# Two attentions moved from beside the branch products into the paired input products of a hybrid decoder layer

## The chip, the cores and the metric

The kernel runs on one core of a Trainium2 chip. The metric is the device time of one execution in microseconds (us); shown are the median and the extremes of three runs, and beside them one further execution that the hardware profiler recorded. Five engines work from queues of their own: PE (matrix products, with PEld for its weight loads), DVE, ACT, POOL, and SP, which here issues every DMA.

## The reference

One decoder layer on x of 1024 tokens by 1024 channels, all in fp32:

```python
h = rms_norm(x, pre_w)
(gdn_qkv, gdn_a, gdn_b, gdn_z, dq, dk, dv, dz, mq, mz, gate_logits) = [h @ w_in[:, lo:hi] for lo, hi in bounds]
...
y_gdn = oa.reshape(b, s, GDN_W).astype(x.dtype) @ w_br_gdn
...
ob = diff_attention_causal(qb, kb, vb, lam, alibi_slopes(DIFF_HEADS))
ob = rms_norm(ob, diff_norm_w) * (1.0 - lam_init)
ob = ob * jax.nn.silu(dz.reshape(b, s, DIFF_HEADS, 2 * DIFF_DH))
y_diff = ob.reshape(b, s, DIFF_W) @ w_br_diff
...
sc = jnp.einsum("bshd,bmhd->bhsm", qc, mk, preferred_element_type=f32) * (MEM_DH ** -0.5)
p = jax.nn.softmax(sc, axis=-1).astype(mv.dtype)
oc = jnp.einsum("bhsm,bmhd->bshd", p, mv).reshape(b, s, MEM_W) * jax.nn.silu(mz)
y_mem = oc @ w_br_mem
gates = jax.nn.sigmoid(gate_logits).reshape(b, s, N_BRANCH, d)
y = gates[:, :, 0] * y_gdn + gates[:, :, 1] * y_diff + gates[:, :, 2] * y_mem
return x + rms_norm(y @ w_out, post_w)
```

Differential attention has 8 heads; each takes two softmaxes (128 query rows against all earlier keys) and subtracts one from the other. Memory attention has 4 heads of 256 channels against 256 memory rows. `oa` comes from a gated delta rule, which is solved in chunks.

## The kernel before

**Stages.** To 600 us: norm of x, the delta rule with its input products, the memory's keys and values. Then `strassen`: all other columns of `h @ w_in` as 36 pairs of 128 columns. A pair is 7 products (order 1, 5, 6, 2, 7, 3, 4) of 12 matmuls 128x512; each fp32 operand is split into a high and a low part (`split`, one ACT cast and one DVE subtraction), and a product is high*high, high*low, low*high. Pair by pair come 8 key/query pairs (`key_query`), 4 of values, 4 of memory queries, 8 under Silu (`plain`, `through`) and 12 under Sigmoid. Results go to DRAM scratch. Key/query pairs also cut their result into halves and parts (`keys_apart`, `queries_apart`).

After the last pair come the branches: `branch(0)` (delta rule), during which differential heads (`diff_side`) run; then the memory heads (`mem_side`) with the heads that are left; then `branch(2)` (memory), again beside heads; `branch(1)` (differential), and the output product with its norm. A branch is 8 `gemm`s of 48 matmuls 128x512, and its 8 inputs are loaded and split (`branch_input`) before its first `gemm`.

**Steps and ticks.** Side work is written as Python generators. `count(n)` is called after n matmuls of the main work; at each `pace[0]` of them, `tick` moves every spawned generator on by one `yield`. So the source is one list of instructions with side work strewn into it, 4 matmuls apart in the branches before. A differential head works on 8 row blocks `i` of width w = 128(i+1): scores (L1051, L1052), bias and row maximum (L1054), `ng` (L1064), two Exp (L1066, L1067), the subtraction (L1069 to L1071), transposes (`turn`, L1086, copied by L1088 and L1090), and the product with the values (L1096). Block i's scores, block i-1's transposes and block i-2's value products follow one another, so three blocks are under way at a time.

**Order.** The framework that builds the kernel takes this list, chooses ahead of the run the order in which each engine gets its instructions, gives them buffers of a pool (`tag`, `bufs`), and adds the waits. Each engine then runs its own list in that order.

Of the kernel before, what the change touches and what calls it, by code (L numbers as in the profile page):

```python
# [50 lines left out]
def hybrid_layer_kernel(  # L51
# [62 lines left out]
    tri = cst([P, P], "tri")  # L114
    G.memset(tri, 1.0)
    G.affine_select(tri, tri, pattern=[[1, P]], compare_op=ALU.is_ge, fill=0.0, base=0, channel_multiplier=-1)
    mneg = cst([P, P], "mneg")
    G.memset(mneg, 0.0)
    G.affine_select(mneg, mneg, pattern=[[1, P]], compare_op=ALU.is_ge, fill=NEG, base=0, channel_multiplier=-1)
    ones = cst([P, P], "ones")  # L120
    G.memset(ones, 1.0)
# [150 lines left out]
    with ExitStack() as gx:  # L272
# [5 lines left out]
        def et(shape=(P, 512), dt=F32):  # L278
            return gp.tile(list(shape), dt, name=nm("e"), tag="e", bufs=3)

# [337 lines left out]
        def scan(h0):  # L618
# [6 lines left out]
            for c in range(8):  # L625
# [9 lines left out]
                for n, h in enumerate(hs):  # L635
                    if c:
                        V.scalar_tensor_tensor(vs[h][:, c], pa[:, n], negeG[:, h, c:c + 1], vs[h][:, c],
                                               op0=ALU.mult, op1=ALU.add)
                    if c < 7:
                        kd[h] = small([P, P], "kd", 2)  # L640
                        A.activation(kd[h], pa[:, 2 + n], AF.Copy, scale=eLG[:, h, c:c + 1])
# [4 lines left out]
                yv = small([P, 2, P], "yv", 2)  # L646
# [11 lines left out]
                for n, h in enumerate(hs):  # L658
                    if c < 7:
                        St[h] = small([P, P], f"St{n}", 2)  # L660
# [38 lines left out]
    def xtile(shape=(P, S), dt=F32):  # L699
        return xp.tile(list(shape), dt, name=nm("x"), tag="x", bufs=6)  # L700
# [3 lines left out]
    mkd = scratch("mkd", 4, (P, 4, MEM))  # L704
    mvd = scratch("mvd", 4, (P, D))
# [97 lines left out]
    class Pair:  # L803


        def __init__(self, cols, put):
            self.cols, self.put = cols, put

# [23 lines left out]
        def multiply(self, p, t):  # L832
            first = p in (1, 5, 2)
            if first:
                ps = sd().rearrange("p a b -> p (a b)")
                self.bank = {**getattr(self, "bank", {}), p: ps}
# [6 lines left out]
            if p in (1, 5, 6):  # L843
                keep = ut()
                A.copy(keep, ps)  # L845
                self.kept = {**getattr(self, "kept", {}), p: keep}
# [21 lines left out]

    def gathered(done):

        got = {}
# [12 lines left out]

    def through(func, dst):

        got = {}

        def put(i, f, ps, add):
            if i not in got:  # L890
                got[i] = xtile()
            t = got[i]
            out_ = t[:, f * 512:f * 512 + 512]
            if add is None:
                A.activation(out_, ps, func)
                A.activation(t[:, 512:], t[:, 512:], func)
            else:
                V.tensor_tensor(out_, ps, add, op=ADD)  # L898
                if i == 0 and f == 1:
                    A.activation(t, t, func)  # L900
            if (i, f) in ((0, 1), (1, 0)):
                nc.sync.dma_start(dst[i], t)
        return put

    LO, HI = slice(0, 64), slice(64, 128)
    kqd = [scratch("kqd", 6, (P, S)) for _ in range(H)]
    vd = scratch("vd", H)
    mqd = [scratch("mqd", 2, (P, S)) for _ in range(8)]
    szd = [scratch("szd", KT) for _ in range(3)]

    def keys_apart(h, t):

        for m, (a, b) in enumerate(((LO, HI), (HI, LO))):
            r = xtile(dt=F32R)
            A.copy(r[a], t[a])
            V.tensor_tensor(r[b], t[a], r[a].bitcast(F32), op=SUB)
            nc.sync.dma_start(kqd[h][m], r.bitcast(F32))
            yield

    def queries_apart(h, t):  # L920


        f = 2.0 ** (h + 1)
        for m, (a, b) in enumerate(((LO, HI), (HI, LO))):
            r = xtile(dt=F32R)
            A.activation(r[a], t[a], AF.Copy, scale=f)
            A.activation(r[b], t[a], AF.Copy, scale=f)
            nc.sync.dma_start(kqd[h][2 + m], r.bitcast(F32))
            yield
            l = xtile(dt=F32R)  # L930
            for c in (a, b):
                V.scalar_tensor_tensor(l[c], t[a], f, r[a].bitcast(F32), op0=MUL, op1=SUB)
            nc.sync.dma_start(kqd[h][4 + m], l.bitcast(F32))
            yield

    def key_query(h):
        return Pair((C_DK + h * P, C_DQ + h * P),
                    gathered(lambda i, t: spawn((queries_apart if i else keys_apart)(h, t))))

    def values_pair(h):  # L940
        return Pair((C_DV + h * P, C_DV + (h + 1) * P),
                    gathered(lambda i, t: nc.sync.dma_start(vd[h + i], t)))

    def mem_query(h):
        def done(i, t):
            hi, lo = xtile(dt=F32R), xtile(dt=F32R)
            split(hi, lo, t)
            nc.sync.dma_start(mqd[2 * h + i][0], hi.bitcast(F32))
            nc.sync.dma_start(mqd[2 * h + i][1], lo.bitcast(F32))
        return Pair((C_MQ + 2 * h * P, C_MQ + (2 * h + 1) * P), gathered(done))  # L950

    def plain(col, n, func, dst):
        return Pair((col + n * P, col + (n + 1) * P), through(func, dst[n:n + 2]))

    def gate(bi, n):
        pg = gemm(w_in, C_G + bi * D + n * P, hh, hl)
        gt = xtile()
        A.activation(gt, pg, AF.Sigmoid)
        nc.sync.dma_start(gts[bi][n], gt)
# [6 lines left out]
    for n in range(2):  # L966
# [3 lines left out]
        for i in range(2):  # L970
            nc.sync.dma_start(mkd[2 * n + i], mk[i].bitcast(F32))
# [380 lines left out]
```

## Time and profile before

| what | us |
|---|---|
| median of 3 runs (lowest, highest) | 1977.41 (1976.53, 1987.22) |
| the profiled execution: its time, its span | 1978.93, 1977.2 |
| busy in the span: PE, DVE, ACT, POOL | 1888.4, 1227.9, 909.4, 215.1 |
| last matmul of the last pair | 1307 |
| branch 0 ends; branch 2 begins; branch 1 begins, ends | 1487; 1610; 1787, 1882 |

The span runs from the first instruction to the last; what the time has beyond it (1.7 us) lies around it. Matmuls overlap in the engine, so what one costs is the distance between starts, not its own length. "Granted clock" is the mean of TensorE's clock as a share of its full rate. Behind a wait stands the instruction that ended it.

### The profile page before, as it was taken

The page shows a single profiled execution, that of the slowest core. Times are in us where ns is not written, and L with a number is a line of the kernel's source. Part 1 is how long each engine was busy: PE and PEld are TensorE (multiplying, and loading weights), DVE is VectorE, ACT ScalarE, POOL GpSimd, SP SyncE. Part 2 cuts the span into 40 slices and gives each one's busy share as a digit, 9 for nine tenths or more (in the row PEclk, how much of TensorE's full clock was granted, in tenths as well). Part 3 has the DMA queues.
Part 4 walks back from the last instruction along what each step waited for, and adds up shares of the span by engine and source line. Part 5 has one row for each costly group of instructions (what it writes and reads, how often), then busy time and mean ns, then how long its engine had stood idle before and what let it go on. Part 6 is the DMA issues. An engine that isn't in the chain of part 4 may idle for free. (4 is left out here: it accounts for less than half of the span.)

```text
span 1977.2 us, 27704 instructions
## 1 busy us (share of the span) xinstructions
PE 1888.4 (96%) x10231; PEld 1575.8 (80%) x10231; DVE 1227.9 (62%) x2422; ACT 909.4 (46%) x1940; POOL 215.1 (11%) x155
## 2 busy tenths in 40 slices
PE   7999999999989999999999999989997799899998
PEld 5778888788877888888888888868886677787786
DVE  5786778754396888556545454547666586774532
ACT  5543563554354666334434444455444464452311
POOL 1230131302100000000000000100001111112211
PEclk9998999999999999999999999989998999999999
DMA  3333131421346666344333323295455666445522
GB/s 125 90 88 99 36 93 44 111 64 54 100 136 203 239 217 225 107 139 163 125 105 108 115 99 127 91 327 193 159 192 177 239 232 233 153 140 202 181 96 85
DMA packets 235259, 282.37 MB, mean 143 GB/s; under 512 B 36994, under 2 KB 176628, under 8 KB 235124
## 3 DMA queue, kind: packets, MB, share of 16 engines
q1 hardware_dynamic: 235124, 280.61, 42.6%
q8 instruction: 80, 1.31, 0.3%
q14 instruction: 55, 0.45, 0.1%
HBM read 189.27 MB, written 91.29 MB: 142 GB/s over the span
## 5 line engine op out<-in xcount | busy, mean ns | idle before, releaser
L840 PE MATMUL sd<-h,y 128*128 128x512 f32 x1296 | 311.8, 389 | 0.0
L840 PEld LDWEIGHTS sd<-h,y 128*128 128x128 f32 x1296 | 243.3, 188 | 50.6
L215 PE MATMUL acc<-h,wh 128*128 128x512 f32 x564 | 238.6, 423 | 8.6 <-ACT h L709 5.5
L216 PE MATMUL acc<-h,wh 128*128 128x512 f32 x564 | 225.2, 400 | 0.5 <-DVE h L710 0.5
L840 PE MATMUL sd<-q,y 128*128 128x512 f32 x864 | 207.5, 389 | 0.0
L840 PE MATMUL sd<-o,y 128*128 128x512 f32 x864 | 201.9, 389 | 0.0
L220 PE MATMUL acc<-h,wl 128*128 128x512 f32 x564 | 191.0, 401 | 0.4 <-DVE wl L165 0.4
L840 PEld LDWEIGHTS sd<-q,y 128*128 128x128 f32 x864 | 162.2, 188 | 33.7
L840 PEld LDWEIGHTS sd<-o,y 128*128 128x128 f32 x864 | 162.2, 188 | 33.7
L163 ACT CAST wh<-wr 128x512 fp32r<-128x512 f32 x144 | 89.2, 619 | 183.3 <-PE acc L216 151.2
L709 ACT CAST y<-wr 128x512 fp32r<-128x512 f32 x148 | 91.9, 622 | 152.8 <-PE sd L840 129.6
L165 DVE TENSOR_TENSOR wl<-wr,wh 128x512 fp32r<-128x512 f32 x144 | 106.8, 744 | 72.3 <-ACT wh L163 59.6
L710 DVE TENSOR_TENSOR y<-y,y 128x512 fp32r<-128x512 f32 x108 | 75.5, 699 | 90.8 <-ACT y L709 90.4
L215 PEld LDWEIGHTS acc<-h,wh 128*128 128x128 f32 x564 | 107.5, 191 | 25.1 <-ACT h L709 6.2
L710 DVE TENSOR_TENSOR y<-wr,y 128x512 fp32r<-128x512 f32 x148 | 103.1, 704 | 33.3 <-ACT y L709 33.1
L220 PEld LDWEIGHTS acc<-h,wl 128*128 128x128 f32 x564 | 104.7, 190 | 21.3 <-DVE wl L165 1.2
L216 PEld LDWEIGHTS acc<-h,wh 128*128 128x128 f32 x564 | 108.0, 192 | 16.5 <-DVE h L710 1.7
L898 DVE TENSOR_TENSOR x<-sd,u 128x512 f32<-128x512 f32 x60 | 41.5, 691 | 89.6 <-PE sd L840 89.6
L1054 DVE CUSTOM_DVE_ANT_0 o<-sd,x 128x512 f32<-128x512 f32 (+3 forms) x128 | 69.4, 569 | 35.9 <-PE sd L1052 35.5
L845 ACT COPY u<-sd 128x512 f32<-128x512 f32 x108 | 63.4, 587 | 60.2 <-PE sd L840 59.5
L991 POOL IOTA ii<- 128x1024 int32 x1 | 1.0, 987 | 728.5 <-DMA gts<-x 728.5
L709 ACT CAST y<-y 128x512 fp32r<-128x512 f32 x108 | 67.0, 621 | 24.4 <-DVE y L710 20.6
(344 smaller groups left out, 3781.0 us busy)
## 6 DMA issues: line engine op xcount, KB each, us to landing
y<-in_w_in_dram SPq DMA_DIRECT2D x144, 256.0 KB, 3.2
kqd<-x SPq DMA_DIRECT2D x48, 512.0 KB, 2.7
wr<-in_w_in_dram SPq DMA_DIRECT2D x64, 256.0 KB, 2.9
y<-kqd SPq DMA_DIRECT2D x32, 512.0 KB, 6.1
gts<-x SPq DMA_DIRECT2D x24, 512.0 KB, 2.7
x<-oscr SPq DMA_DIRECT2D x24, 512.0 KB, 4.7
x<-gts SPq DMA_DIRECT2D x24, 512.0 KB, 4.3
o<-gscr SPq DMA_DIRECT2D x16, 512.0 KB, 4.4
```

The lines of the kernel that those rows point to most:

```text
L163: A.copy(hi, raw)
L165: V.tensor_tensor(lo, raw, hi.bitcast(F32), op=ALU.subtract)
L215: T.matmul(ps[:, sl], lhsT=hi[:, kk], rhs=hh(k, f), start=(k == 0), stop=False)
L216: T.matmul(ps[:, sl], lhsT=hi[:, kk], rhs=hl(k, f), start=False, stop=False)
L220: T.matmul(ps[:, sl], lhsT=lo[:, kk], rhs=hh(k, f), start=False, stop=(k == 7))
L709: A.copy(hi, src)
L710: V.tensor_tensor(lo, src, hi.bitcast(F32), op=SUB)
L840: T.matmul(ps, lhsT=t[:, l, kk], rhs=comb[p][kk][r], start=(first and kk + n == 0), stop=(kk == 3 and n == 2), skip_group_check=True)
L845: A.copy(keep, ps)
L898: V.tensor_tensor(out_, ps, add, op=ADD)
L991: G.iota(ii, pattern=[[1, S]], base=-896, channel_multiplier=-1)
L1054: V.tensor_tensor_reduce(s[i][m][:, u:e], ps[m], base[:, off + u:off + e], 1.0, NEG if u == 0 else mx[:, 0, m:m + 1], op0=ALU.add, op1=ALU ...
```

## The change

Each differential head and each memory head becomes one generator without the three-block overlap, `diff_head` and `mem_head`, with single steps a `yield` or `pause(2)` apart. One generator, `attention`, runs all 12 heads after each other, and is spawned ahead of `strassen`, whose pace becomes 3 matmuls a tick, so that heads run between the products of the pairs. The pairs are put in another order: keys and queries of a head, then either values or a Silu pair, so that head h finds its inputs when it starts; a Silu pair now stands beside every second head, and all Sigmoid pairs come last. Outputs of pairs are handled by halves of 512 columns (`ut` buffers) in place of whole 1024-column tiles; queries and memory keys lie in DRAM so that a row block is one load. Two banks of a pair come from `acc`. Heads work in seven `x` buffers (six before), for which small constants move to a pool that is freed.

The three branches then follow with no attention beside them, in the order 0, 1, 2. `make0` prepares the first three inputs of branch 0 behind the last head and the rest when the pairs are done; `make1` runs beside branch 0, `make2` beside branch 1. Two elementwise steps move from POOL to DVE: the branches' sum, and the memory softmax's scaling. The head-independent `base` and `nlam` are made before the pairs.

```diff
...
     xp = ctx.enter_context(pool("xp"))
 
     def xtile(shape=(P, S), dt=F32):
-        return xp.tile(list(shape), dt, name=nm("x"), tag="x", bufs=6)
+        return xp.tile(list(shape), dt, name=nm("x"), tag="x", bufs=7)
...
             first = p in (1, 5, 2)
-            if first:
-                ps = sd().rearrange("p a b -> p (a b)")
-                self.bank = {**getattr(self, "bank", {}), p: ps}
+            if p == 1:
+                both = acc()
+                self.bank[1], self.bank[5] = both[:, :512], both[:, 512:]
+            elif p == 2:
+                self.bank[2] = sd().rearrange("p a b -> p (a b)")
             ps = self.bank[{1: 1, 6: 1, 7: 1, 4: 1, 5: 5, 3: 5, 2: 2}[p]]
...
+    LO, HI = slice(0, 64), slice(64, 128)
+    kd2 = [scratch("kd2", 2) for _ in range(H)]
+    qd = scratch("qd", H, (P, NT, 4, P))
...
+    def mark(*key):
+        parts[key] = parts.get(key, 0) + 1
...
         def put(i, f, ps, add):
-            if i not in got:
-                got[i] = xtile()
-            out_ = got[i][:, f * 512:f * 512 + 512]
+            t = ut()
             if add is None:
-                A.copy(out_, ps)
+                A.copy(t, ps)
             else:
-                V.tensor_tensor(out_, ps, add, op=ADD)
-            if (i, f) in ((0, 1), (1, 0)):
-                done(i, got[i])
+                V.tensor_tensor(t, ps, add, op=ADD)
+            done(i, f, t)
         return put
+    def through(func, dst, name):
+
 
         def put(i, f, ps, add):
-            if i not in got:
+            t = ut()
-                A.activation(out_, ps, func)
-                A.activation(t[:, 512:], t[:, 512:], func)
+                A.activation(t, ps, func)
+                V.tensor_tensor(t, ps, add, op=ADD)
+                A.activation(t, t, func)
+            nc.sync.dma_start(dst[i][:, half[f]], t)
+            mark(name, i)
         return put
...
+    def keys_apart(h, f, t):
 
         for m, (a, b) in enumerate(((LO, HI), (HI, LO))):
-            r = xtile(dt=F32R)
+            r = ut(dt=F32R)
...
+    def queries_apart(h, f, t):
+
+
+        g = 2.0 ** (h + 1)
...
-            r = xtile(dt=F32R)
-            A.activation(r[a], t[a], AF.Copy, scale=f)
-            A.activation(r[b], t[a], AF.Copy, scale=f)
-            nc.sync.dma_start(kqd[h][2 + m], r.bitcast(F32))
-            l = xtile(dt=F32R)
+            r = ut(dt=F32R)
+            A.activation(r[a], t[a], AF.Copy, scale=g)
+            A.activation(r[b], t[a], AF.Copy, scale=g)
+            store(m, r)
+            yield
...
+        for h in range(2):
+            for u in range(2):
+                nc.sync.dma_start(mkd[2 * n + h][:, :, u], mk[u][:, 2 * h:2 * h + 2].bitcast(F32))
...
-    strassen([key_query(h) for h in range(H)]
-             + [values_pair(h) for h in range(0, H, 2)]
-             + [mem_query(h) for h in range(4)]
-             + [plain(C_DZ, n, AF.Silu, szd[1]) for n in range(0, 8, 2)]
-             + [plain(C_MZ, n, AF.Silu, szd[2]) for n in range(0, 8, 2)]
-             + [plain(C_G + b * D, n, AF.Sigmoid, gts[b]) for b in (1, 2, 0) for n in range(0, 8, 2)])
-    flush()
...
-    def diff_loads(h):
-        ks = [yt(dt=F32R) for _ in range(2)]
-        qh = [yt(dt=F32R) for _ in range(2)]
-        ql = [qt(dt=F32R) for _ in range(2)]
-        for t, src in zip(ks + qh + ql, kqd[h]):
-            nc.sync.dma_start(t.bitcast(F32), src)
-        return ks, qh, ql
...
+    def diff_head(h):
+        yield from wait(lambda: all(parts.get((c, h), 0) == 2 for c in "kqv"))
+
+        ks = [xtile(dt=F32R) for _ in range(2)]
+        for m in range(2):
+            nc.sync.dma_start(ks[m].bitcast(F32), kd2[h][m])
+        def load_queries(i):
+            qs[i] = wp.tile([P, 4, P], F32R, name=nm("wl"), tag="wl", bufs=2)
+            nc.sync.dma_start(qs[i].bitcast(F32), qd[h][:, i])
...
+        yield from pause(4)
+        vt = xtile((P, 8, P))
...
+        for i in range(NT):
+            if i + 1 < NT:
+                load_queries(i + 1)
+            q4 = qs.pop(i)
+            mx = small([P, 2, 2], "mx", 4)
             if w <= 512:
-                both = ot((P, 2, 512))
-                s[i] = [both[:, 0], both[:, 1]]
+                s2 = xtile((P, 2, 512))
+                s = [s2[:, 0], s2[:, 1]]
+                s = [xtile(), xtile()]
...
+                    T.matmul(ps[m], lhsT=q4[:, m], rhs=ks[m][:, u:e], start=True, stop=False)
+                    T.matmul(ps[m], lhsT=q4[:, 2 + m], rhs=ks[m][:, u:e], start=False, stop=True)
...
+                yield
             ng = small([P, 2], "ng", 4)
-            V.tensor_scalar(ng, mxs[i][:, (w - 1) // 512], -scl, None, op0=ALU.mult)
+            V.tensor_scalar(ng, mx[:, (w - 1) // 512], -scl, None, op0=MUL)
+            yield
-            A.activation(s0[:, :w], s0[:, :w], AF.Exp, bias=ng[:, 0:1], scale=scl, accum_out=l0[:, i:i + 1])
-            A.activation(s1[:, :w], s1[:, :w], AF.Exp, bias=ng[:, 1:2], scale=scl, accum_out=l1)
+            A.activation(s[0][:, :w], s[0][:, :w], AF.Exp, bias=ng[:, 0:1], scale=scl, accum_out=l0[:, i:i + 1])
+            A.activation(s[1][:, :w], s[1][:, :w], AF.Exp, bias=ng[:, 1:2], scale=scl, accum_out=l1)
+            yield from pause(2)
             c1 = small([P, 1], "c1", 4)
             V.reciprocal(c1, l1)
-            V.scalar_tensor_tensor(c1, c1, l0[:, i:i + 1], nlam, op0=ALU.mult, op1=ALU.mult)
-            V.scalar_tensor_tensor(s0[:, :w], s1[:, :w], c1, s0[:, :w], op0=ALU.mult, op1=ALU.add)
-
+            V.scalar_tensor_tensor(s[0][:, :w], s[1][:, :w], c1, s[0][:, :w], op0=MUL, op1=ADD)
+            yield from pause(2)
+
+            pT = s[1].rearrange("p (a b) -> p a b", b=P)
+            for b in range(0, i + 1, 4):
...
+                yield
+            yield
             po = sd()
             for c in range(i + 1):
                 T.matmul(po[:, 0], lhsT=pT[:, c], rhs=vt[:, c], start=(c == 0), stop=(c == i))
+            yield
             A.copy(o[:, i], po[:, 0])
-        for i in range(NT + 2):
-            if i < NT:
-                yield from scores(i)
-                weights(i)
-                if i:
-                    yield
-            if i == 1:
-                vt = ot()
-                tokens(vt, 0)
-                tokens(vt, 1)
-                o = ot()
-            if 1 <= i <= NT:
-                turn(i - 1, 0)
-                yield
...
-        ready.add(("diff", h))
+        G.tensor_tensor(o, o, bc(sso, P), op=MUL)
+        yield from wait(lambda: parts.get((("sz", 1, h // 2), h % 2), 0) == 2)
         yield from pause(5)
...
-
-    def branch_input(bi, news):
+                split(*(pT[mt][:, u, sl] for u in range(2)), src)
+            yield from pause(2)
+            if i2 % 2:
+                for d in range(2):
...
+    def branch_input(bi, news, at=0):
 
         got = []
+
+        def steps():
+            for n in range(KT):
+                if bi == 0 and n == 3:
+                    yield from wait(lambda: "pairs" in ready)
+                hi, lo = (new((P, S), F32R) for new in news[2 * n:2 * n + 2])
+                for sl in half:
+                    raw = ut()
+                    nc.sync.dma_start(raw, oscr[bi][n][:, sl])
+                    yield
+                    split(hi[:, sl], lo[:, sl], raw)
+                got.append((hi, lo))
+                yield
+        return got, steps()
+
+    in0, make0 = branch_input(0, [xtile] * 6 + [ht] * 10)
+
+    def attention():
+        for h in range(H):
+            yield from diff_head(h)
+        for h in range(4):
+            yield from mem_head(h)
+        ready.add("attention")
+        yield from make0
+    pairs = []
+    for h in range(H):
+        pairs.append(key_query(h))
+        pairs.append(silu_z(1, C_DZ, h - 1) if h % 2 else values_pair(h))
+    for h in range(4):
+        pairs.append(mem_query(h))
+        pairs.append(silu_z(2, C_MZ, 2 * h))
+    pairs += [gates(b, n) for b in range(3) for n in range(0, KT, 2)]
+
+    spawn(attention())
+    pace[0] = 3
+    strassen(pairs)
+    ready.add("pairs")
+    pace[0] = 6
+    until(lambda: "attention" in ready)
...
+                spawn(sides.pop(0))
+            t = ot((P, S))
...
+            pb = gemm(w_b, n * P, part(0), part(1))
+            V.tensor_tensor(t, pb, t, op=MUL)
             if not first:
-                G.tensor_tensor(t, t, yp_, op=ALU.add)
+                V.tensor_tensor(t, t, yp_, op=ADD)
...
-    wide = [ht] * 12 + [qt] * 4
-    pace[0] = 4
-    for h in range(H):
-        spawn(diff_side(h))
-    branch(0, w_bg, branch_input(0, wide), first=True)
-    spawn(mem_side())
-    until(lambda: ("om", 3) in ready)
-    branch(2, w_bm, branch_input(2, wide))
-    flush()
...
-    pace[0] = 6
-    branch(1, w_bd, branch_input(1, [yt, ot] * 8), last=True, beside=out_weights)
+    in1, make1 = branch_input(1, [qt] * 8 + [yt] * 8)
+    in2, make2 = branch_input(2, [ht] * 12 + [xtile] * 4)
+    branch(0, w_bg, in0, first=True, beside=[make1])
+    branch(1, w_bd, in1, beside=[make2])
+    branch(2, w_bm, in2, last=True, beside=[pause(1), out_weights()])
     flush()
```

## Rows read from the trace of the kernel before

**Rows 1.** The page, parts 1 and 2: busy time, and slices of 49.4 us.
```profile
PE 1888.4 (96%) x10231; PEld 1575.8 (80%) x10231; DVE 1227.9 (62%) x2422; ACT 909.4 (46%) x1940; POOL 215.1 (11%) x155
...
PE   7999999999989999999999999989997799899998
...
PEclk9998999999999999999999999989998999999999
```
**Rows 2.** Busy time by stretch: length, engines, granted clock, DMA share, GB/s.
```profile
622.90:1307.10 684.20, 684.20 (x3018) 566.47 (x3019) 407.10 (x561) 318.59 (x494) 6.43 (x4) 1.00 0.43 149
1307.10:1325.00 17.90, 10.73 (x35) 7.31 (x34) 9.93 (x27) 12.00 (x20) 0.00 (x0) 0.71 0.99 368
1325.00:1487.00 162.00, 155.36 (x899) 132.81 (x899) 109.15 (x306) 80.17 (x229) 10.67 (x6) 1.00 0.53 190
1487.00:1610.00 123.00, 100.73 (x596) 84.03 (x597) 79.74 (x235) 59.49 (x195) 21.41 (x18) 0.93 0.56 195
1610.00:1787.50 177.50, 166.90 (x961) 141.38 (x959) 128.09 (x312) 90.68 (x239) 30.29 (x13) 0.99 0.56 195
1787.50:1882.50 95.00, 91.17 (x397) 74.16 (x396) 44.57 (x50) 24.84 (x39) 25.15 (x10) 0.98 0.57 195
```
**Rows 3.** Waits of PE from 1307 to 1882.5 us: total, times, longest.
```profile
PE sd L1086 <- DVE o L1071: 14.5, 10, 3.2
PE acc L215 <- ACT h L709: 5.5, 2, 5.3
PE sd L1188 <- POOL u L1180: 5.3, 2, 2.9
```
**Rows 4.** Timeline of two neighbouring products of a pair: start, length, instruction.
```profile
1298.97 2.88 PE L840 MATMUL sd<-q,y 128*128 128x512 f32 x12
...
1301.69 2.88 PE L840 MATMUL sd<-h,y 128*128 128x512 f32 x12
```
**Rows 5.** Timeline: two instructions that stand ahead of their place in the source.
```profile
601.38 0.40 PE L840 MATMUL sd<-h,y 128*128 128x512 f32 x1
...
1296.82 0.41 SPq L1021 DMA_DIRECT2D u<-szd  x1
```
**Rows 6.** ACT's timeline where pairs and attention meet, and its table loads by line.
```profile
1309.04 0.20 ACT L1003 ACTIVATE l<-l 128x2 f32<-128x2 f32 x1 [1.28 <-DVE l L1002]
1309.26 1.28 ACT L895 ACT_TABLE_LOAD   x1
1310.56 0.60 ACT L895 ACTIVATE x<-sd 128x512 f32<-128x512 f32 x1
1311.17 1.28 ACT L1066 ACT_TABLE_LOAD   x1
...
L423 ACT ACT_TABLE_LOAD x13 | 16.7, 1283 | 15.9 <-DVE v L421 8.1 <-DVE y L421 7.6
L452 ACT ACT_TABLE_LOAD x12 | 15.4, 1283 | 0.2
```
**Rows 7.** Busy time of three more stretches, columns as in rows 2.
```profile
25.00:550.00 525.00, 514.56 (x3543) 435.91 (x3541) 350.22 (x777) 257.71 (x599) 96.93 (x66) 0.98 0.27 75
650.00:800.00 150.00, 150.00 (x663) 124.21 (x662) 123.26 (x157) 92.51 (x129) 0.00 (x0) 1.00 0.59 213
...
1800.00:1875.00 75.00, 74.12 (x323) 60.12 (x322) 33.01 (x37) 20.24 (x30) 18.08 (x7) 1.00 0.63 212
```
**Rows 8.** Timeline of one row block, w = 768, beside branch 0.
```profile
1389.34 0.39 PE L1051 MATMUL sd<-y,y 128*128 128x512 f32 x1
...
1395.27 1.02 DVE L1071 SCALAR_TENSOR_TENSOR o<-o,c,o 128x768 f32<-128x768 f32 x1
...
1400.26 0.60 PE L1086 MATMUL sd<-ident,o 128*128 128x128 f32 x4
1400.94 0.59 ACT L1088 COPY o<-sd 128x512 f32<-128x512 f32 x1 [3.33 <-PE sd L1086]
```
**Rows 9.** Groups of instructions: an add and a product of the sizes that change engine.
```profile
L1241 DVE TENSOR_TENSOR x<-acc,x 128x1024 f32<-128x1024 f32 x24 | 29.3, 1220 | 9.8 <-PE acc L220 9.7
L1243 POOL TENSOR_TENSOR x<-x,x 128x1024 f32<-128x1024 f32 x16 | 42.8, 2675 | 158.8 <-DVE x L1241 109.6 <-DVE ng L1064 38.9 <-DVE c L1069 10.4
```

More of the change, by code (lines that the diff above doesn't have):

```diff
@@ L1191, in turn @@
                 sl = slice(i2 % 2 * 256, i2 % 2 * 256 + 256)
-                split(*(pT[i2 // 2][mt][:, u, sl] for u in range(2)), src)
-        def products(f):
-            for d in range(2):
-                cs = slice(h * 256 + d * P, h * 256 + (d + 1) * P)
-                po = sd().rearrange("p a b -> p (a b)")
-                for mt in range(2):
-                    for u, v in PASSES:
-                        T.matmul(po, lhsT=mv[mt][u][:, cs], rhs=pT[f][mt][:, v],
-                                 start=(mt + u + v == 0), stop=(mt + u == 2))
-                scaled(2, 2 * h + d, f, po)
-                yield
@@ L1205, in mem_head @@
-        for i2 in range(6):
-            if i2 < 4:
-                scores(i2)
-                yield
-            if i2 >= 2:
-                turn(i2 - 2)
-                yield
-            if i2 in (4, 5):
-                yield from products(i2 - 4) if i2 == 4 else products(1)
-        ready.add(("om", h))
-    def branch_input(bi, news):
-        got = []
-        for n in range(KT):
-            raw = xtile()
-            nc.sync.dma_start(raw, oscr[bi][n])
-            hi, lo = (new((P, S), F32R) for new in news[2 * n:2 * n + 2])
-            split(hi, lo, raw)
-            got.append((hi, lo))
-        return [lambda k, f, i=i: got[k][i][:, f * 512:f * 512 + 512] for i in range(2)]
@@ L1228, in hybrid_layer_kernel @@
-    yh, yl = [], []
-    def branch(bi, w_b, inputs, first=False, last=False, beside=None):
-        for n in range(KT):
-            if n == 4 and beside:
-                spawn(beside())
-            t = xtile()
+                split(*(pT[mt][:, u, sl] for u in range(2)), src)
+            yield from pause(2)
+            if i2 % 2:
+                for d in range(2):
+                    cs = slice(d * P, (d + 1) * P)
+                    po = sd().rearrange("p a b -> p (a b)")
+                    for mt in range(2):
+                        for u, v in PASSES:
+                            T.matmul(po, lhsT=mv[:, mt, u, cs], rhs=pT[mt][:, v],
+                                     start=(mt + u + v == 0), stop=(mt + u == 2))
+                    yield from wait(lambda: parts.get((("sz", 2, h), d), 0) == 2)
+                    scaled(2, 2 * h + d, i2 // 2, po)
+                    yield
@@ L1236, in branch @@
+    pairs += [gates(b, n) for b in range(3) for n in range(0, KT, 2)]
[5 more added lines that the diff above has]
+    until(lambda: "attention" in ready)
+    yh, yl = [], []
+    def branch(bi, w_b, got, first=False, last=False, beside=()):
+        sides = list(beside)
+        for n in range(KT):
+            if n % 2 == 0 and sides:
+                spawn(sides.pop(0))
+            t = ot((P, S))
             nc.sync.dma_start(t, gts[bi][n])
@@ L1237, in branch, with part, get @@
             if not first:
-                yp_ = xtile()
+                yp_ = ot((P, S))
                 nc.sync.dma_start(yp_, yscr[n])
-            pb = gemm(w_b, n * P, *inputs)
-            V.tensor_tensor(t, pb, t, op=ALU.mult)
+            def part(u):
+                def get(k, f):
+                    until(lambda: len(got) > k)
+                    return got[k][u][:, half[f]]
+                return get
+            pb = gemm(w_b, n * P, part(0), part(1))
+            V.tensor_tensor(t, pb, t, op=MUL)
```

300 lines of the change are left out of this document (134 added, 166 removed).

## The prediction

> **What bounds the kernel now.** I read the page first: PE is busy for 1888.4 of 1977.2 us, and its row of slices has its only low digits at the two ends and in the last third, where the granted clock dips as well [rows 1]. The busy time by stretch says where the rest goes [rows 2]. Through the pairs, 622.9 to 1307.1 us, PE is busy for all of 684.2 us at clock 1.00, while DVE has 407.1 us of work and ACT 318.6. The attention that follows, 1307.1 to 1787.5, is another picture: PE idles for 7.17 + 6.64 + 22.27 + 10.60 = 46.7 us, 22 of them between branch 0 and branch 2, where heads run with no branch beside them. The waits name the chain inside a row block: transposes L1086 stand 14.5 us for the subtraction L1071, and a branch's first matmul stands 5.5 us for its input's cast L709 [rows 3]. So PE sets the time nearly everywhere, and what can be won is its idle time in the attention, with the clock that idling costs.
>
> **What PE must do.** Two neighbouring products of 12 matmuls start 1301.69 - 1298.97 = 2.72 us apart, 0.227 us a matmul [rows 4]. A branch of 384 is then 87.0 us. Attention took 480.4 us, of which two branches are 174.1 and idling 46.7; 259.6 us remain for the heads' own matmuls. Part of that is low clock: busy time times the missing clock in the four stretches (0.29, 0, 0.07, 0.01) is 3.1 + 7.1 + 1.7 = 11.9 us [rows 2]. The heads' matmuls are thus about 248 us at full clock (an estimate). Branch 1 takes 95.0 us for its 87.0. No matmul is added, removed or given another shape: queries only lie elsewhere. If PE never stood still again after 622.9 us, the span would be 1977.2 - 46.7 - 11.9 - 8.0 = 1910.6 us. That ceiling, 66.6 us, is all this change can bring.
>
> **The change, part by part.**
>
> *Heads between the products.* The pairs have 36 x 28 = 1008 ticks of three matmuls, 0.68 us each. By the source a differential head takes 4 + 2 + 4 x 9 + 4 x 11 + 8 = 94 ticks and a memory head 39, together 908. Head 0 can start when two pairs are done, tick 56, so the last head ends at tick 964 of 1008: 44 ticks, 30 us, to spare. The new stretch has 684 + 248 = 932 us of PE work. Its DVE work is at most 407 + 327 = 734 us, 79%; 327 is all that DVE did from 1307.1 to 1787.5, two branches included [rows 2], which is more than the few microseconds that the halved instructions and the memory scaling add. ACT has at most 319 + 242 = 561 us, 60%, before table loads.
>
> *Table loads.* Exp now alternates with Silu and Sigmoid. Where pairs and attention met once before, ACT made two loads of 1.28 us around a single Sigmoid, and the cast behind each load began at once; in the delta rule 25 loads by two lines did the same [rows 6]. In the new order 20 pairs have four outputs each, 4 ticks apart. 64 row blocks in 752 ticks put an Exp into such a gap in 0.34 of cases, and nearly always ahead of a pair's first: 2.0 switches a pair, 41 there and 41 back, 82 x 1.283 = 105 us more for ACT, which is then 71% busy. The delta rule's stretch bounds what this does to PE: with its 25 loads PE idled 10.4 of 525 us [rows 7], 0.42 us a load if all of it were theirs, so 34 us for 82.
>
> The Trainium skill ("ScalarE: Activation LUTs", sections "What ACT_TABLE_LOAD costs" and "Table sets: the hidden batching unit") tells to batch activations by table set and gives 2.66 us for a switch, a drain of 1.38 us included. By it ACT would have 218 us of switches and be 84% busy. The trace agrees with the load's 1.28 us and shows no drain behind it.
>
> *Stalls in the new stretch.* Three rows bound the share of time for which PE stands in such a mixture: 0% in the key/query pairs, though DVE was 82% busy there; 2.0% in the delta rule [rows 7]; 4.1% in branch 0 and 6.0% in branch 2 with heads beside them [rows 2]. So 0 to 56 us of 932. I take 3%, 28 us: the mixture resembles the delta rule (chains, three functions on ACT) but is fuller. The fullest part is the key/query pairs: DVE had 15.6 us a pair of 19.0 [rows 7], and 28 ticks of heads add 10.1, so 25.7 us of 26.7.
>
> What decides whether the small steps suffice is the chain in a block. For w = 768 it took 6.95 us from the first score to the end of the subtraction, and the transposes then waited for their place until 1400.26 [rows 8]. With transposes, their copy and the value products I estimate 10.1 us in all; the source now allots 11 ticks, 7.5 us, plus the block's own 3.8 us on PE. That leaves 1.2 us for queues. Nor is a late step at once a stall: a product of a pair ran among the memory matmuls at 601.38, and a load of `szd` was issued at 1296.82, a whole head ahead of its use [rows 5]. The order on an engine is made ahead with products pulled forward.
>
> *Head of branch 0.* It had 5.5 us of waiting and a clock of 0.71 [rows 2, 3]. With three inputs ready, 18 matmuls, 4.1 us, cover the load of the next; I take 4 us of idling, from 0 to 7.
>
> *Branches alone.* Their inputs are made beside the branch before. The pure stretch of branch 1 idled 0.88 of 75 us, 1.2% [rows 7]: 3 us for 261. The sum on DVE instead of POOL costs DVE 16 x 1.22 us [rows 9], hidden behind matmuls, since DVE was busy for only 33 of 75 us there [rows 7]; without that cover it would cost 19.5 us. It removes POOL's 2.7 us from the path between `gemm` and store.
>
> *Costed at nothing.* More but smaller DMAs (some 150 issues of about 0.4 us on SP, whose longest neighbours are loads made a pair ahead; DMA share 0.43 in the pairs, 0.5 to 0.6 in attention [rows 2]); the two banks of `acc`; constants in another pool; `base` on POOL, made 38 us ahead of its first use. For DVE standing behind the load of `lv`, and for the smaller stores of memory keys, I put 2 us. If the DMA cover failed, a late key load (not bounded by a stall here) would lengthen a head, which is rival B.
>
> **Sum.** 1910.6 + 28 + 4 + 3 + 2 = 1947.6 us of span, 29.6 less. The profiled execution's time was 1.7 us above its span and 1.5 us above the median, so the median comes to 1948 us. A change under about 0.5% (10 us) can't be told from none here, as the three runs alone spread by that.
>
> **The rivals.**
>
> *A. Table loads stop PE.* The place is the Exp of a block: a load of 1.28 us takes the whole 1.2 us that the chain can spare, and the casts of the next products stand behind it on ACT. If PE waited one load at each of 41 Exp switches, stalls would be 53 us (1972 in all); at all 82, 105 us (2025). It makes the kernel slower from 67 us of stalls, 0.8 us a load. For it: the order made ahead put two loads around one Sigmoid [rows 6]. Against: at most 0.42 us a load in the delta rule. Middle price 2000. The rule of the Trainium skill on batching ("ScalarE: Activation LUTs", "Table sets: the hidden batching unit") speaks for this case.
>
> *B. Attention outlasts the pairs.* 30 us to spare over 64 blocks is 0.47 us a block. If queues add 1.7 us to a block beyond its ticks, heads end 79 us late, and branch 0 can't begin, because its first inputs need the heads' `x` buffers. Alone, PE works 3.8 of a block's 10.1 us, so 62% of 79 us, 49 us, is idle: 1997. For it: 96% of DVE's time in the key/query pairs, and two buffers fewer for scores than the old overlap used. Against: the old heads kept their pace in branch 0 with PE 96% busy.
>
> *C. The stall only moves.* PE stands at branch 2's rate, 6.0%: 56 us, 1976. No change. For it: the same wait, transposes for the subtraction, leads the waits now [rows 3], and blocks no longer overlap. Against: that stretch had POOL's slow sums beside it.
>
> *D. Better than forecast.* 0 to 1% of stalls: 1920 to 1929.
>
> **How the numbers follow.** My forecast (stalls of 1.5 to 4.5%) has 0.54, D 0.12, C 0.15, A 0.09, B 0.10. Faster is forecast and D, 0.66; same is C, 0.15; slower A and B, 0.19. The range from 1918 to 1994 leaves out part of A and B and the best end of D, 2 in 10; the forecast's own range is 1934 to 1962.
>
> **What would show it.** Right: the stretch of pairs ends near 1560 to 1590 us with PE 97% busy and clock near 1.00, about 80 table loads in it, heads ended before the last pair, and three branches of some 88 us behind. Wrong by A: waits of PE on Exp's successors with a table load ahead of them, over 0.8 us each. Wrong by B: Exp or value products after the last product of a pair, and low clock there. Wrong by C: waits of transposes spread over the whole stretch, totalling over 50 us. Key/query pairs with PE under 95% would mean DVE.

## The result, and the profile after

The change makes the kernel slower: 2085.68 us median of 4 runs (2083.08 to 2088.94), against 1978.07 (1976.53 to 1987.22); the ratio is 1.0535, 95% interval 1.0499 to 1.0570. The prediction was 1948, faster. The profiled execution after took 2085.42 us, with a span of 2083.7.

The page, parts 1 and 2, of the kernel after, to be held against [rows 1]:

```profile
PE 1933.1 (93%) x10231; PEld 1579.0 (76%) x10231; DVE 1248.0 (60%) x2534; ACT 1019.7 (49%) x2114; POOL 156.3 (8%) x123
...
PE   7999999999989888898889899899998998999998
...
PEclk9999999999999999999999999999999999999999
```

PE has the same 10231 matmuls. The dip in the last third of [rows 1] is gone; in its place PE misses a tenth in many slices from the fourteenth on. The slices lie where the pairs are, and the windows give the size. Busy time by stretch after: the pairs with the heads between them, the three branches, the last stage:

```profile
622.90:1717.00 1094.10, 988.81 (x4752) 794.47 (x4753) 674.38 (x1445) 625.30 (x1274) 30.62 (x16) 0.97 0.47 148
1717.00:1988.00 271.00, 264.70 (x1140) 215.19 (x1139) 117.96 (x147) 69.16 (x111) 0.00 (x0) 0.99 0.60 194
...
1988.00:2083.70 95.70, 87.97 (x387) 72.14 (x385) 27.86 (x37) 12.94 (x35) 14.74 (x16) 0.98 0.26 89
```

Against the ceiling of the prediction (932, 261 and 94.7 us) that is 162.1 us too long in the first, 10.0 in the second and 1.0 in the third; the three make up the 173.1 us by which the span exceeds 1910.6. The loss is in the pairs. There PE idles 105.3 us; the other 57 us sit inside "busy". Some 30 of them are low clock, reckoned as in the prediction (988.8 us at a missing clock of 0.03, an estimate). At the end of the first head, for example, PE was busy for 3.69 of the 7.80 us to 764.8, and then the granted clock was 0.50, the lower of its levels of 1.2 and 2.4 GHz:

```profile
764.80:771.60 6.80, 6.02 (x22) 5.32 (x23) 4.02 (x5) 1.72 (x4) 0.72 (x1) 0.50 0.68 207
```

The rest, some 27 us, is short stalls: a matmul is shown 389 ns and more long but follows the one before it in 227 ns [rows 4], so a stall shorter than the difference widens the spacing and leaves no idle time to see.

The waits of PE in that stretch (total, times, longest) name who was late:

```profile
PE acc L847 <- ACT u L852: 49.2, 32, 4.7
PE sd L1124 <- POOL x L1118: 18.1, 7, 6.0
PE sd L1100 <- DVE x L1092: 11.7, 12, 3.9
PE sd L1109 <- ACT x L1102: 8.3, 13, 1.0
PE acc L847 <- DVE u L895: 6.8, 9, 2.5
```

The first line is new: before, PE was busy for all of the 684.2 us of the pairs [rows 2]. L847 is the matmul of a product and L852 the copy `A.copy(self.kept[p], ps)` out of its bank. One such place in the timeline:

```profile
1668.75 0.39 PE L847 MATMUL acc<-h,y 128*128 128x512 f32 x1
...
1669.61 1.28 ACT L1160 ACT_TABLE_LOAD   x1
1670.90 0.47 ACT L1160 ACTIVATE wh<-sd,mmx 128x256 f32<-128x256 f32 x1
...
1671.82 0.58 ACT L852 COPY u<-acc 128x512 f32<-128x512 f32 x1
...
1672.45 0.96 PE L847 MATMUL acc<-o,y 128*128 128x512 f32 x2 [3.32 <-ACT u L852]
```

The product that starts at 1672.45 writes one bank, the copy before it reads the other, and PE stands 3.32 us until the copy is through. ACT does the copy late, behind a table load and Exps of a head. Both banks are halves of one tile, `both = acc()`. That became the theory: the order between writing and reading holds for the whole tile, so a product waits for the reading of the other half, which the kernel before, with a tile for each bank, never had to. The rivals were A (table loads) and B and C in the form "the chain in a head is too slow for its steps".

### The profile page after: what moved, and what is told of

It reads as the page before. It is cut to its first block, busy times and chain, and to the rows that moved or that the text cites. A ratio compares the mean times of both kernels' runs of the same rounds, so it can differ in the third digit from the quotient of the medians.

```text
span 2083.7 us, 28447 instructions
## 1 busy us (share of the span) xinstructions
PE 1933.1 (93%) x10231; PEld 1579.0 (76%) x10231; DVE 1248.0 (60%) x2534; ACT 1019.7 (49%) x2114; POOL 156.3 (8%) x123
## 4 chain that ended last, share of the span: by engine, by line
PE 50%; issue 33%; DVE 7%; DMA 4%; ACT 4%; POOL 2%; SPq 0%; ACTq 0%; POOLq 0%; DVEq 0%
PE acc L847 9%; PE acc L207 9%; PE acc L212 8%; PE acc L208 8%; PE sd L847 2%; PE sd L1306 1%; PE sd L462 1%; PE sd L1151 1%; DMA wr<-in_w_mem_kv_dram 1%; PE sd L649 1%; PE sd L1184 1%; DVE wl L157 1%; POOL x L1118 1%; PE sd L661 1%; PE sd L656 1%
## 5 line engine op out<-in xcount | busy, mean ns | idle before, releaser
L847 PE MATMUL acc<-o,y 128*128 128x512 f32 x864 | 246.1, 427 | 47.4 <-ACT u L852 47.2
L847 PEld LDWEIGHTS acc<-o,y 128*128 128x128 f32 x864 | 168.0, 204 | 94.7 <-ACT u L852 62.6
L847 PE MATMUL acc<-q,y 128*128 128x512 f32 x864 | 225.5, 401 | 10.2 <-DVE u L895 6.4
L847 PE MATMUL acc<-h,y 128*128 128x512 f32 x864 | 223.8, 398 | 1.4 <-DVE u L907 0.9
L847 PEld LDWEIGHTS acc<-q,y 128*128 128x128 f32 x864 | 157.3, 189 | 50.5 <-DVE u L895 10.5
L847 PEld LDWEIGHTS acc<-h,y 128*128 128x128 f32 x864 | 158.0, 189 | 38.7 <-DVE u L907 5.1
L847 PE MATMUL sd<-h,y 128*128 128x512 f32 x432 | 116.2, 400 | 0.9 <-ACT y L713 0.9
L1078 DVE CUSTOM_DVE_ANT_0 x<-sd,x 128x512 f32<-128x512 f32 (+3 forms) x128 | 68.9, 571 | 54.7 <-PE sd L1076 54.3
L852 ACT COPY u<-acc 128x512 f32<-128x512 f32 x108 | 63.0, 583 | 77.8 <-PE acc L847 77.5
L847 PEld LDWEIGHTS sd<-h,y 128*128 128x128 f32 x432 | 78.6, 189 | 16.4 <-ACT y L713 1.3
```

The costliest lines, as they stand in the source:

```text
L847: T.matmul(ps, lhsT=t[:, l, kk], rhs=comb[p][kk][r], start=(first and kk + n == 0), stop=(kk == 3 and n == 2), skip_group_check=True)
L852: A.copy(self.kept[p], ps)
L1078: V.tensor_tensor_reduce(s[m][:, u:e], ps[m], base[:, off + u:off + e], 1.0, NEG if u == 0 else mx[:, 0, m:m + 1], op0=ADD, op1=ALU.max, a ...
```

## The experiments

**1. A tile for each bank.** On the changed kernel; `acc` has two tiles, and each bank now takes half of one.

```diff
-            if p == 1:
-                both = acc()
-                self.bank[1], self.bank[5] = both[:, :512], both[:, 512:]
+            if p in (1, 5):
+                self.bank[p] = acc()[:, :512]
```

> The changed kernel, but a pair's two accumulators (products 1, 6, 7, 4 and products 5, 3) lie in two `acc` tiles, half of each unused, not in the two halves of one. Theory T (one tile): in the changed kernel a product into one half waits until the other half has been read, so 49.2 us of PE's waits on the copy L852 and 9.5 us on the sums L895 and L907 go, with low clock behind them: 2005 to 2030 us, and no wait of over 1 us on L852. Rival A (ACT is late by table loads and Exp): product 6 waits for the copy of product 1 as late as before, so the waits stay: 2070 to 2090 us. Rival B (the heads' chain): the same 2070 to 2090 us, for the pairs only fill in.

Measured: 2008.08 us (2003.71 to 2020.55), ratio to the kernel before 1.0171 (1.0130 to 1.0211). The one edit gives back 78 of the 108 us (72 by the two ratios to the kernel before). The wait for the copy falls from 49.2 to 1.9 us. The waits for the sums, which theory T wanted gone as well, do not fall: 9.5 us in the changed kernel, 20.6 here. Waits of PE from 622.9 us to the end of the pairs in this run (copy of a product L851, sums of products L894 and L906):

```profile
PE sd L1123 <- POOL x L1117: 16.4, 8, 3.2
PE acc L846 <- DVE u L894: 11.6, 7, 3.9
PE acc L846 <- DVE u L906: 9.0, 3, 3.6
PE sd L1099 <- DVE x L1091: 7.7, 10, 2.2
...
PE acc L846 <- ACT u L851: 1.9, 3, 1.1
```

**2. One tile in the kernel before.** The same edit backwards, with no heads between the products.

```diff
-            if first:
-                ps = sd().rearrange("p a b -> p (a b)")
-                self.bank = {**getattr(self, "bank", {}), p: ps}
+            if p == 1:
+                both = acc()
+                self.bank = {1: both[:, :512], 5: both[:, 512:]}
+            elif p == 2:
+                self.bank[2] = sd().rearrange("p a b -> p (a b)")
```

> The kernel before with one part of the change alone: a pair's two accumulators are the halves of one `acc` tile. No heads run beside the pairs. Theory T: PE, which was busy for all of 684 us of the pairs, now waits for L845-like copies and for the sums: 10 to 60 us more, 1990 to 2040 us, unless the order made ahead hides all of it. Rivals A and B: no change, 1975 to 1982 us, since nothing makes ACT late here.

Measured: 2029.57 us (2027.87 to 2032.01), ratio 1.0259 (1.0241 to 1.0278). The pairs, with no heads beside them, end at 1359 instead of 1307. The edit costs 51 us where ACT has no work of a head. (It also takes the two banks from another pool; experiments 1 and 11 change the tile alone.) Busy time of the pairs, against the first line of [rows 2]:

```profile
622.90:1359.00 736.10, 717.18 (x3023) 552.36 (x3021) 397.84 (x572) 314.02 (x495) 6.55 (x4) 1.00 0.41 139
```

PE's "busy" grew by 33 us for the same matmuls at a clock of 1.00, its idle time by 19: most of this stall would be missed by whoever looks for PE's idle time only. The waits of the weight loads in the same stretch (copy of a product L847, sums L900 and L882, cast of weights L709) show it:

```profile
PEld acc L842 <- ACT u L847: 25.9, 78, 1.1
PEld sd L842 <- ACT y L709: 19.2, 28, 0.8
PEld acc L842 <- DVE x L900: 14.4, 40, 2.3
PEld acc L842 <- DVE x L882: 9.8, 32, 0.4
```

That is 78 waits for copies and 72 for sums in 36 pairs, about two of each a pair, as theory T has it: products 5 and 6 wait for copies, 3 and 4 for sums. In the kernel before, weight loads wait twice in the whole stretch of the pairs, for 1.2 us, and neither time for such a reading. The 28 waits for the cast of product 2's weights came with the edit too; why stays open.

**3. No table loads.** The changed kernel with Copy in place of Silu and Sigmoid in the pairs (so the gates are not computed).

```diff
-                A.activation(t, ps, func)
+                A.activation(t, ps, AF.Copy)
...
-                A.activation(t, t, func)
+                A.activation(t, t, AF.Copy)
```

> The changed kernel with Silu and Sigmoid of the pairs left out (their results are copied instead), so Exp is the only table function beside the pairs: some 75 table loads fewer, 96 us of ACT. Rival A: 50 us or more go, 2035 us or less, and the waits on L852 shrink by half. Theory T: the waits on L852 shrink a little, since copies come less late; 2055 to 2080 us. Rival B: 2070 to 2085 us.

Measured: 2054.45 us (2053.82 to 2055.08), ratio 1.0384 (1.0358 to 1.0410), at the lower edge of what theory T said. 31 us come back, and PE still stands 37.2 us, 34 times, for the copies of products. The loads cost something, but they are not the main cause; rival A falls as the explanation of the loss.

**4. Heads behind the pairs.** `spawn(attention())` of the changed kernel moved behind `strassen(pairs)`.

> The changed kernel with the attention spawned behind the pairs, so the pairs run alone in their new form and the heads run bare, one after the other, ahead of branch 0. Theory T: the pairs alone take more than their 685 us, 700 to 745 us, with waits on L852, L895 and L907. Rivals A and B: 685 us, PE never idle. For all: the bare heads show their chain, one head after the other with nothing to fill it; from my estimate of a block, 10 us for w = 768, some 65 us a differential head and 30 us a memory head, 640 us for 248 us of matmuls, so the whole takes 2280 to 2400 us.

Measured: 2562.17 us, one run; longer than all theories said. Its two stretches, pairs alone and bare heads:

```profile
622.90:1372.00 749.10, 725.42 (x3047) 555.66 (x3047) 415.50 (x630) 337.13 (x580) 5.51 (x3) 1.00 0.45 139
1372.00:2200.00 828.00, 442.77 (x1729) 367.59 (x1728) 278.72 (x828) 216.23 (x634) 28.32 (x16) 0.62 0.23 73
```

Pairs without heads are 65 us longer than before, against the 52 of experiment 2; where the other 13 come from stays open. The bare heads are the surprise: PE idles nearly half the time, the granted clock falls to 0.62 (between the levels of 1.2 and 2.4 GHz), and transposes stand 260.0 us, 64 times, for the subtraction. So the small steps do hide a very long chain, and the cover is worth far more than I had thought.

**5 to 8. What is left above the kernel before.** Experiment 1 is still 1.7% slower than the kernel before. Its waits name POOL's product at a head's end; its windows show the same. Two neighbouring windows of experiment 1, with a head's end (two POOL instructions) and without:

```profile
1131.00:1168.00 37.00, 31.56 (x159) 25.93 (x159) 22.33 (x52) 16.76 (x41) 3.53 (x2) 0.95 0.46 143
1168.00:1205.00 37.00, 35.78 (x177) 28.69 (x176) 23.00 (x58) 23.69 (x50) 0.00 (x0) 1.00 0.46 142
```

Three edits, each on experiment 1, and two of them together. The heads' ends:

```diff
-        G.tensor_tensor(o, o, bc(sso, P), op=MUL)
         yield from wait(lambda: parts.get((("sz", 1, h // 2), h % 2), 0) == 2)
-        yield from pause(5)
+        sz = [scale_of(1, h, b) for b in range(2)]
+        yield from pause(4)
+        V.tensor_tensor(o, o, bc(sso, P), op=MUL)
+        yield from pause(3)
```

> On top of the change with two separate banks (2008 us). The end of a differential head: the product of the output with its norms goes from POOL to DVE, ahead of it four steps of pause and behind it three, and the two loads of the gate are issued seven steps before their use. In the run with separate banks PE stood 16.4 us for POOL's product, in 8 waits, and the stretches of 37 us that hold a head's end had PE busy for 31 us where the others have 36; DVE stood 8.9 us for the gate's load. Theory E (heads' ends are what is left): all of some 5 us in each of eight heads comes back, 30 to 45 us, 1965 to 1980. Theory F (the waits only move on to the next thing that is late, DVE's queue): under 12 us, 1996 to 2008, with waits on DVE's copies and sums longer.

Tanh in place of Sigmoid, `0.5 + 0.5 * tanh(z / 2)`, and of Silu, `z * (1 + tanh(z / 2))` with the half of it moved into the scales of the heads; DVE's part runs in `finish`, two steps later:

```diff
-                A.activation(t, t, func)
+                A.activation(t, t, AF.Tanh, scale=0.5)
...
+            yield from pause(2)
+            if z is None:
+                V.tensor_scalar(t, t, 0.5, 0.5, op0=MUL, op1=ADD)
+            else:
+                V.scalar_tensor_tensor(t, t, 1.0, z, op0=ADD, op1=MUL)
```

> On top of the change with two separate banks (2008 us). Sigmoid and Silu of the pairs are computed from Tanh, with one more instruction of DVE for each output, two steps later; the result is the same function. If Tanh stands in the table set of Exp, the 76 loads in the stretch fall to a few. Theory A (loads cost PE some 0.4 us each, as the run of the change without them showed): 20 to 32 us come back, 1976 to 1988. Theory F (loads lay in ACT's idle time; the 80 more instructions of DVE, some 40 to 55 us, cost as much): 2000 to 2015.

Both:

> Both edits, the end of the heads on DVE with early loads of the gate, and Tanh for Sigmoid and Silu, on the change with two separate banks (2008 us). If the two causes are separate, their gains add: 1935 to 1970, which would be below the kernel before (1978). If both are forms of one cause (DVE's and ACT's queues are full), the sum is less than the larger of the two plus 5 us: 1970 to 2000.

One step of pause moved, in each row block, from behind the transposes to behind the Exps:

```diff
-            yield from pause(2)
+            yield from pause(3)
             c1 = small([P, 1], "c1", 4)
...
                 yield
-            yield
             po = sd()
```

> On the change with two separate banks (2008 us). One step of pause in each row block moves from behind the transposes to behind the two Exps, so that DVE's reciprocal is issued 0.7 us later. DVE stood 50 us at that reciprocal for Exp, with the reads of finished products behind it. Theory Q (DVE's queue stands there and PE's late banks, 20 us of waits on DVE's sums, come from it): those waits halve, 1985 to 2000. Theory S (DVE has time, and the step taken from the value products makes PE wait for the copies of the transposes): no gain or a loss, 2005 to 2025.

Measured on one chip (kernel before 1975.79, 19 runs):

| kernel | us (lowest, highest) | ratio to before, 95% interval |
|---|---|---|
| heads' ends | 1971.50 (1969.12, 1973.63) | 0.9972 (0.9960, 0.9984) |
| Tanh | 1977.06 (1970.50, 1979.77) | 0.9992 (0.9974, 1.0011) |
| both | 1956.77 (1954.23, 1961.14) | 0.9908 (0.9877, 0.9938) |
| pause moved | 1993.58 (1991.21, 1994.82) | 1.0085 (1.0061, 1.0110) |

Heads' ends give 37 us, Tanh 31, both 51: less than the sum of 68, so they share a part, but more than either alone. All these gains are counted from experiment 1, four runs on another chip that spread by 17 us, so each is known to some 8 us only. The first edit cut PE's waits for the product at a head's end from 16.4 to 3.0 us, and those for DVE's sums from 20.6 to 7.4. The pause gives 14 us (by the two intervals 4 to 30); PE's waits for DVE's sums fell with it from 20.6 to 14.2 us, a third and not the half that theory Q said, so its mechanism is only partly shown. The loads did go with Tanh: from 613 us on, ACT's row by line in the Tanh run has one load left, and that one stands at 619.5 us, ahead of the pairs' stretch,

```profile
L1014 ACT ACT_TABLE_LOAD x1 | 1.3, 1283 | 0.0
```

where the changed kernel has 77 in its pairs, against the two of [rows 6] where pairs and attention met once:

```profile
L908 ACT ACT_TABLE_LOAD x33 | 42.3, 1283 | 0.6
L1086 ACT ACT_TABLE_LOAD x23 | 29.5, 1283 | 1.2 <-DVE ng L1083 0.8
L1160 ACT ACT_TABLE_LOAD x15 | 19.2, 1283 | 18.0 <-DVE mmx L1155 17.9
L905 ACT ACT_TABLE_LOAD x6 | 7.7, 1283 | 0.2 <-issue 0.2
```

The Trainium skill ("ScalarE: Activation LUTs", section "Table sets: the hidden batching unit") lists tanh in the set of exp and in that of sigmoid; the trace agrees, Tanh and Exp alternated without a load.

**9. Everything together.** Heads' ends, Tanh, the moved pause, and with them early loads of the memory heads' gate, two more steps behind POOL's power and one behind the memory heads' Exp:

```diff
+            if i2 % 2:
+                yield from wait(lambda: parts.get((("sz", 2, h), 1), 0) == 2)
+                sz = [scale_of(2, 2 * h + d, i2 // 2) for d in range(2)]
...
-            yield
+            yield from pause(2)
             V.reciprocal(lm, lm)
...
-        yield from pause(4)
+        yield from pause(6)
         V.tensor_tensor(o, o, bc(sso, P), op=MUL)
```

> All that helped, on the change with two separate banks: heads' ends on DVE, Tanh for Sigmoid and Silu, the step of pause moved behind the Exps, and with them what DVE's waits in the run of the two together still name (12.4 us for the gate's load of the memory heads, 12.1 us for POOL's power, 15.2 us for the memory heads' Exp): the memory heads' gate is loaded ahead, two more steps stand behind POOL's power and one more behind the memory heads' Exp. If DVE's standing queue is what is left, 10 to 20 us below the run of the two together (1956.8): 1937 to 1947. If PE's remaining idle time doesn't come from DVE's queue, 1952 to 1958. If the 32 steps more make the heads outlast the pairs, over 1960.

Measured: 1956.22 us (1952.15 to 1957.15), ratio 0.9881 (0.9855 to 0.9907) to the kernel before. No better than the two edits, and the pause that gave 14 us alone adds nothing: the second theory holds, what is left is not DVE's queue. Busy time of its pairs with the heads, and of its branches:

```profile
622.90:1578.70 955.80, 940.54 (x4744) 775.01 (x4744) 705.54 (x1528) 527.76 (x1200) 13.53 (x9) 1.00 0.53 167
1578.70:1855.00 276.30, 269.89 (x1153) 217.67 (x1154) 123.75 (x156) 73.38 (x116) 0.00 (x0) 0.98 0.61 197
```

PE idles 15.3 us in the first, 1.6%. Against the ceiling this kernel loses 23.8 us in the pairs and 15.3 in the branches, 5.2 of these in three waits of branch 0's first matmuls for the casts of their inputs.

**10. The heads' ends in the kernel before.** The edit of experiment 5 there, with two steps of pause ahead of the product in place of four.

> The kernel before, with the one edit of the heads' end alone: the product with the norms on DVE, the gate loaded ahead. It tells what that edit is worth without the change. If heads' ends cost PE in any order, by 8 heads of some 5 us, 1945 to 1960. If it is the small steps between products that make DVE's and POOL's standing visible to PE, as the waits of the kernel before say (none on POOL's product among the three longest), within 6 us of the kernel before: 1970 to 1982.

Measured: 1975.82 us (1971.07 to 1980.11), ratio 0.9983 (0.9966 to 1.0000). 2.5 us, by the interval at most 7: beside branches a late head's end held up little, between products it cost 37.

**11. One tile again.** The kernel of experiment 7 with `both = acc()` back.

> The run of the two edits together (heads' ends on DVE, Tanh), with the two banks in one tile again as the change has them. If the price of one tile stands by itself, as in the kernel before (51 us) and in the change (78 us), it is 50 to 80 us here too: 2007 to 2037. If it cost so much only because ACT's copies stood behind table loads, 15 to 40 us: 1972 to 1997.

Measured: 2035.25 us (2034.44 to 2038.03), ratio 1.0284 (1.0255 to 1.0314), 78 us above experiment 7 (1956.77). Its first wait of PE:

```profile
PE acc L848 <- ACT u L853: 37.5, 36, 4.5
```

One tile costs 78 us here too, with the table loads of Silu and Sigmoid gone. It needs no load to make the copies late.

## Why the prediction was wrong

**The step that failed** is in "Costed at nothing": "the two banks of `acc`". I had looked at this edit as a change of place, and named no work that hides it. It is an added wait: products 5 and 6 of a pair wait for ACT's copy, and products 3 and 4 for DVE's sum, out of the other bank. In the kernel before the product after a copy goes to another tile, and PE has 2.72 us, one product [rows 4], while the copy runs. Experiments 1 and 11 measure it with the heads between (78 us each), experiment 2 without (51 us). The trace could have led there: [rows 7] says that the key/query pairs had PE 100% busy with DVE at 82%, so the pairs live off the slack between a product and the reading of its bank, and the diff removes that slack. That this wait exists is shown by experiment 2's weight loads, 150 waits where there were none; that the framework makes it because it keeps order for a tile as a whole is inferred, since no run shows its list of waits. Of the other things costed at nothing, the DMAs held: in the pairs PE waited for a load once, for 1.1 us.

**Stalls of 3%, 28 us, with 0 to 6% as bounds.** This term failed as well. Without the shared tile, experiment 1 takes 1013.1 us for the 932, 81 us more, and the bound was 56:

```profile
622.90:1636.00 1013.10, 958.30 (x4746) 784.86 (x4746) 669.72 (x1447) 624.58 (x1275) 30.95 (x17) 0.98 0.51 159
```

PE idles 54.8 us of it, 5.4%, near the rate of rival C, and some 19 us more are low clock (958.3 us at a missing 0.02, an estimate), which the term left out. The mixture did resemble branch 2 more than the delta rule. With its 2008.08 us this kernel would have missed the forecast too. Only with all of experiment 9's repairs does idling come to 1.6% and the stretch to 955.8 us, against the forecast's 960; that they lie so close says nothing for the sum, which was made for another kernel.

**Table loads.** 82 forecast, 77 counted; 34 us forecast for them if all of the delta rule's idling were theirs, 31 measured, by Copy with one tile and by Tanh with two. The count was right; the price, 0.40 us a load, was right partly by luck, since nothing showed that the delta rule idled for its loads alone. And I had let the 34 us vanish in 28 for all stalls together. Rival A's mechanism was real at half its price of decision (0.8 us a load); its waits behind loads occur at the copies (the timeline at 1669.61), and without loads they remain. The Trainium skill's price for a switch ("ScalarE: Activation LUTs", section "What ACT_TABLE_LOAD costs") has a drain of 1.38 us in it; in the timeline the activation starts 1.29 us after its load starts, which leaves no room for one.

**The heads' ends** were not a term of the sum. POOL's power and product take 3.8 us (1.79 and 2.01 in experiment 1), and the source leaves five steps, 3.4 us, for both and for the sums on DVE ahead of them. PE then waits 2.1 us on average, and the gate's load, issued beside its use, holds up DVE with the next products' sums behind it. By experiment 5 that is 37 us of 8 heads, by experiment 10 hardly anything where branches lie beside them. I had counted the steps of a block, not those of an end.

**Attention done in time (B).** Right: the last matmul of the heads starts at 1680 in a stretch that ends at 1717, 37 us to spare (forecast 30). **Rival C** in its own form fails: transposes wait 11.7 us for the subtraction, not over 50. What experiment 4 adds is why the small steps are needed at all.

**Heads' matmuls, 248 us.** PE is busy for 940.5 us in the pairs of experiment 9 where I had 932; the estimate is low by 9 us at most.

**Branches alone.** 271.0 us, forecast 268. The head of branch 0 and the inputs made beside other branches cost what was said, and the sum on DVE stayed hidden. The front is the same (by 622.9 us PE had started 3950 matmuls before and 3956 after), and the last stage took 95.7 us against 94.7.

**The ceiling** of 1910.6 stands: no run went below it, and the best closes 22 of its 66.6 us.

What stays open: of the 108 us, 72 to 78 are the shared tile's. How the 30 us that are left divide can't be said exactly, since heads' ends and loads gain 68 singly and 51 together, and the change's own gains lie under them.

## What to carry to other kernels

When an edit moves two accumulators into one tile, cost it as a wait: ask of each instruction that writes one half who reads the other, and how late that reader can be. PE's 100% in a stage that alternates between banks is made by that slack, and a stage without idle time is the worst place to take it from. Side work cut into small steps needs its steps counted to its very end, slow engines and loads included, because between products every late step also holds back the main work's own copies and sums in the same queues.

## What the runs showed that was not expected

A stall can be invisible as idle time: in experiment 2, 52 us of lengthening showed as 19 us of idling and 33 us more "busy" for the same matmuls, and the waits of the weight loads named who was late. Tanh and Exp alternate without a table load, and Sigmoid and Silu made from Tanh with one more instruction of DVE each gave 31 us. Heads with nothing beside them ran at a mean granted clock of 0.62 and took some 820 us to the branches, where between products their matmuls add some 256 us (940.5 less the pairs' 684).
